# A softmax over 32768 columns on one core: other rows per partition, other statistics, other DMA pieces

## The chip, the core and the metric

One of the eight cores of a Trainium2 chip runs the whole program. The time is device microseconds (us) from start to end of one execution. Before the change, ten executions gave a median of 2504.91 us, from 2501.88 to 2509.04 us.

Names used below: DVE is the vector engine, ACT the scalar engine, SP the engine that issues the DMAs here, and a DMA is a transfer between the chip's main memory and the on-chip memory of 128 partitions. A DMA is carried out by 16 DMA engines at once.

## The reference

```python
batch, seq, vocab = 16, 256, 32768          # logits, float32; temperature = 1.0
scaled = logits / temperature
scaled = scaled - scaled.max(axis=-1, keepdims=True)
exp_scaled = np.exp(scaled)
return (exp_scaled / exp_scaled.sum(axis=-1, keepdims=True)).astype(np.float32)
```

There are 4096 rows of 32768 numbers, 128 KB each: 536.87 MB to read and as much to write.

## The kernel before

The input is cut into 128 tiles of 4 MB. A tile is 32 whole rows: each row is cut into four quarters of 8192 columns, and each quarter (32 KB) lies on one partition, so partition p of a tile holds the p-th stretch of 32 KB of 4 MB that are contiguous in main memory. `_BUFS` = 6 such tiles fit on the chip at once.

`load` (L49 to L54) and `store` (L56 to L59) each issue one DMA of 4 MB from SP's queue. `keep_in_program_order` fixes their order to what the last loop writes (L134 to L140): four loads (`_AHEAD` = 4), then, for each tile, its store and the load of the tile four later. SP works through its queue in this order, so a DMA that has to wait holds back all later ones. A load waits until the store that last used its buffer has landed; a store waits until the tile is finished.

`compute` (L74 to L132) works on a tile in two chunks of 4096 columns (`NCH` = 2):

- DVE finds the negated maximum of each chunk (L87), and ACT computes the exponential of the chunk in place with that maximum, and its sum on the way (L94).
- The small part (L103 to L125) joins the two chunks of a partition and then the four partitions of a row. `combine` (L61 to L72) does the latter in `n_rounds` = 2 rounds of a shuffle among 32 partitions (L64) and a `tensor_tensor` (L67); it is called once for the maximum and once for the sum. ACT computes the correcting exponentials (L106), DVE the weighted sum (L113) and the reciprocal (L124), and ACT the final factors (L125).
- The chunk is multiplied by its factor: of eight chunks in turn three on DVE (L130) and five on ACT (L132).

Which engine does which work is written out in the code. The order within DVE's and ACT's queues is set by a scheduler, and the small part is marked `high_priority`.

Of the kernel before, what the change touches and what calls it, by code (L numbers as in the profile page):

```python
# [1 line left out]

# [4 lines left out]


_W = 8192
_BUFS = 6  # L10
_AHEAD = 4
_CC = 4096
_SCALE_ON_DVE = {1, 4, 7}


@with_exitstack
def kernel(
    ctx: ExitStack,
    tc: tile.TileContext,
    logits: bass.AP,  # L20
    temperature: bass.AP,
    out: bass.AP,
):
    nc = tc.nc
    inv_t = 1.0 / float(temperature)
    P = nc.NUM_PARTITIONS
    fp32 = mybir.dt.float32
    Exp = mybir.ActivationFunctionType.Exp
    Copy = mybir.ActivationFunctionType.Copy
    X = mybir.AxisListType.X  # L30
    A = mybir.AluOpType

    xf = logits.flatten_outer_dims()
    of = out.flatten_outer_dims()
    N, V = xf.shape
    W = min(_W, V)
    SPLIT = V // W
    assert SPLIT * W == V and (N * SPLIT) % P == 0 and W % _CC == 0
    x = xf.rearrange("n (h v) -> (n h) v", h=SPLIT)
    o = of.rearrange("n (h v) -> (n h) v", h=SPLIT)  # L40
    n_tiles = N * SPLIT // P
    n_rounds = SPLIT.bit_length() - 1
    NCH = W // _CC

    xpool = ctx.enter_context(tc.tile_pool(name="x", bufs=_BUFS))
    spool = ctx.enter_context(tc.tile_pool(name="stats", bufs=8))
    slots = {}

    def load(t: int) -> None:  # L49
        xs = xpool.tile([P, W], fp32, tag="x", name="xs")  # L50
        slots[t] = xs
        tc.keep_in_program_order(
            nc.sync.dma_start(out=xs, in_=x[t * P : (t + 1) * P, :])
        )  # L54

    def store(t: int) -> None:  # L56
        tc.keep_in_program_order(
            nc.sync.dma_start(out=o[t * P : (t + 1) * P, :], in_=slots.pop(t))  # L58
        )  # L59

    def combine(v, op) -> None:  # L61
        for j in range(n_rounds):
            mask = [i ^ (1 << j) for i in range(32)]
            nc.vector.stream_shuffle(  # L64
                out=v[:, j + 1 : j + 2], in_=v[:, j : j + 1], mask=mask
            )
            nc.vector.tensor_tensor(  # L67
                out=v[:, j + 1 : j + 2],
                in0=v[:, j : j + 1],
                in1=v[:, j + 1 : j + 2],  # L70
                op=op,
            )  # L72

    def compute(t: int) -> None:  # L74
        xs = slots[t]
        nm = spool.tile([P, NCH], fp32, tag="nm", name="nm")
        ssum = spool.tile([P, NCH], fp32, tag="ssum", name="ssum")
        ee = spool.tile([P, NCH], fp32, tag="ee", name="ee")
        f = spool.tile([P, NCH], fp32, tag="f", name="f")
        ttj = spool.tile([P, NCH], fp32, tag="ttj", name="ttj")  # L80
        nMh = spool.tile([P, 1 + n_rounds], fp32, tag="nMh", name="nMh")
        Sh = spool.tile([P, 1 + n_rounds], fp32, tag="Sh", name="Sh")
        rS = spool.tile([P, 1], fp32, tag="rS", name="rS")

        for c in range(NCH):
            xc = xs[:, c * _CC : (c + 1) * _CC]
            nc.vector.tensor_reduce(  # L87
                out=nm[:, c : c + 1], in_=xc, axis=X, op=A.max, negate=True
            )
            if inv_t != 1.0:  # L90
                nc.vector.tensor_scalar_mul(
                    out=nm[:, c : c + 1], in0=nm[:, c : c + 1], scalar1=inv_t
                )
            nc.scalar.activation(  # L94
                out=xc,
                in_=xc,
                func=Exp,
                bias=nm[:, c : c + 1],
                scale=inv_t,
                accum_out=ssum[:, c : c + 1],  # L100
            )

        with tc.high_priority():  # L103
            nc.vector.tensor_reduce(out=nMh[:, 0:1], in_=nm, axis=X, op=A.min)  # L104
            combine(nMh, A.min)
            nc.scalar.activation(  # L106
                out=ee,
                in_=nm,
                func=Exp,
                bias=nMh[:, n_rounds : n_rounds + 1],  # L110
                scale=-1.0,
            )
            nc.vector.tensor_tensor_reduce(  # L113
                out=ttj,
                in0=ee,
                in1=ssum,
                scale=1.0,
                scalar=0.0,
                op0=A.mult,
                op1=A.add,  # L120
                accum_out=Sh[:, 0:1],
            )
            combine(Sh, A.add)
            nc.vector.reciprocal(out=rS, in_=Sh[:, n_rounds : n_rounds + 1])  # L124
            nc.scalar.activation(out=f, in_=ee, func=Copy, scale=rS)  # L125

        for c in range(NCH):
            xc = xs[:, c * _CC : (c + 1) * _CC]
            if (t * NCH + c) % 8 in _SCALE_ON_DVE:
                nc.vector.tensor_scalar_mul(out=xc, in0=xc, scalar1=f[:, c : c + 1])  # L130
            else:
                nc.scalar.activation(out=xc, in_=xc, func=Copy, scale=f[:, c : c + 1])  # L132

    for t in range(min(_AHEAD, n_tiles)):  # L134
        load(t)
    for t in range(n_tiles):
        compute(t)
        store(t)
        if t + _AHEAD < n_tiles:
            load(t + _AHEAD)  # L140


# [1 line left out]
_INS = ['logits', 'temperature']  # L144
_OUTS = [((16, 256, 32768), 'float32')]

_NUMBERS = {'temperature': 1.0}


# [26 lines left out]
```

## Time and profile before

| what | before |
|---|---|
| median of ten executions | 2504.91 us |
| the profiled execution's own time | 2509.04 us |
| its span, from the first instruction to the last | 2507.3 us |
| instructions | 4102 |
| maximum of 128x4096, DVE (L87) | 4414 ns, 256 times |
| exponential of 128x4096, ACT (L94) | 3707 ns, 256 times |
| multiplication of 128x4096, ACT (L132) | 3705 ns, 160 times |
| multiplication of 128x4096, DVE (L130) | 2353 ns, 96 times |
| one load or store | 4096 KB, 128 of each |
| one packet of a DMA engine | 32768 bytes, 1213 ns (median) |

The span is what the trace covers; the execution's own time is 1.7 us longer. The profiled execution is also the slowest of the ten, 4.1 us above their median. In a line of the costliest groups the name is followed by the tiles that are written and read, the shape, the count, the busy time in us, the mean of one in ns, and the idle time of the engine just before such an instruction, with what ended it. In a line of waits, the engine and line that waited stand to the left of the arrow, and what they waited for to its right. Every DMA consists of packets[...], and the trace has the start and the length of each packet. It also has the moment at which each of the 16 DMA engines finished its part of a DMA.

### The profile page before, as it was taken

The numbers are of one execution on the slowest core, as the hardware profiler recorded it, in microseconds if no ns is written. First come the engines' busy times: TensorE is split into PE (matmuls) and PEld (weight loads), VectorE is DVE, ScalarE is ACT, GpSimd is POOL, SyncE is SP. The second block draws the span as 40 slices with busy tenths as digits, with TensorE's granted clock in tenths as the row PEclk, the third lists the DMA queues.
The fourth block names the chain that finished last, engine by engine and source line by source line (L and its number), as shares of the span: only waits on it lengthen the run. The fifth ranks groups of instructions, "written<-read, shape, count | busy, mean of one in ns | idle before, by whom it ended". The sixth has DMA issues, their size and how long they took to land.

```text
span 2507.3 us, 4102 instructions
## 1 busy us (share of the span) xinstructions
DVE 1564.3 (62%) x2400; ACT 1624.9 (65%) x929; POOL 0.2 (0%) x4
## 2 busy tenths in 40 slices
DVE  6666566666566666666666666566666666666664
ACT  6766666666666666666666666666666666666664
POOL 0000000000000000000000000000000000000000
DMA  9999999999999999999999999999999999999996
GB/s 410 432 433 434 431 432 433 435 434 431 433 433 433 434 432 431 434 434 434 432 431 434 432 434 431 431 434 433 435 431 432 434 434 434 432 431 435 432 434 273
DMA packets 36896, 1074.02 MB, mean 428 GB/s; under 512 B 4096, under 2 KB 4096, under 8 KB 4096
## 3 DMA queue, kind: packets, MB, share of 16 engines
q1 hardware_dynamic: 36864, 1073.76, 99.3%
q14 instruction: 32, 0.26, 0.0%
HBM read 536.87 MB, written 536.87 MB: 428 GB/s over the span
## 4 chain that ended last, share of the span: by engine, by line
DMA 73%; DVE 12%; ACT 9%; another core or an unknown queue 5%; issue 0%; SPq 0%; ACTq 0%
DMA xs<-in_logits_dram 47%; DMA out_dram<-xs 25%; DVE nm L87 10%; ACT xs L94 4%; ACT xs L132 4%; DVE Sh L67 0%; DVE Sh L64 0%; ACT f L125 0%; DVE xs L130 0%; ACT ee L106 0%; DVE rS L124 0%; DVE ttj L113 0%; SPq L58 0%; DVE nMh L67 0%
## 5 line engine op out<-in xcount | busy, mean ns | idle before, releaser
L87 DVE TENSOR_REDUCE nm<-xs 128x1 f32<-128x4096 f32 x256 | 1119.6, 4414 | 439.2 <-DMA xs<-in_logits_dram 439.2
L94 ACT ACTIVATE xs<-xs,nm 128x4096 f32<-128x4096 f32 x256 | 949.1, 3707 | 684.1 <-DVE nm L87 684.1
L132 ACT ACTIVATE xs<-xs,f 128x4096 f32<-128x4096 f32 x160 | 589.9, 3705 | 4.1
L113 DVE CUSTOM_DVE_ANT_0 ttj<-ee,ssum 128x2 f32<-128x2 f32 x128 | 20.5, 160 | 391.7 <-ACT ee L106 383.1
L130 DVE TENSOR_SCALAR xs<-xs,f 128x4096 f32<-128x4096 f32 x96 | 225.9, 2353 | 41.0 <-ACT f L125 41.0
L125 ACT ACTIVATE f<-ee,rS 128x2 f32<-128x2 f32 x128 | 37.8, 295 | 159.1 <-DVE rS L124 159.1
L94 ACT ACTIVATION_READ_ACCUMULATOR xs<-xs,nm 128x1 f32 x256 | 47.7, 187 | 0.0
L67 DVE TENSOR_TENSOR nMh<-nMh 128x1 f32<-128x1 f32 x256 | 40.8, 159 | 8.6
L67 DVE TENSOR_TENSOR Sh<-Sh 128x1 f32<-128x1 f32 x256 | 40.8, 159 | 8.6
L64 DVE STREAM_SHUFFLE nMh<-nMh 128x1 f32<-128x1 f32 x256 | 38.8, 151 | 0.0
L64 DVE STREAM_SHUFFLE Sh<-Sh 128x1 f32<-128x1 f32 x256 | 38.8, 151 | 0.0
L106 ACT ACTIVATE ee<-nm,nMh 128x2 f32<-128x2 f32 x128 | 35.8, 280 | 0.0
L124 DVE RECIPROCAL rS<-Sh 128x1 f32<-128x1 f32 x128 | 21.0, 164 | 4.3
L104 DVE TENSOR_REDUCE nMh<-nm 128x1 f32<-128x2 f32 x128 | 19.8, 155 | 4.3
L113 DVE DVE_READ_ACCUMULATOR2_ANT Sh<- 128x1 f32 x128 | 10.6, 83 | 0.0
L64 DVE LOAD_MASK_SELECT Sh<-Sh x256 | 3.6, 14 | 10.8
L64 DVE LOAD_MASK_SELECT nMh<-nMh x256 | 3.6, 14 | 10.7
L94 ACT ACT_TABLE_LOAD x1 | 1.3, 1283 | 12.9 <-DMA xs<-in_logits_dram 12.9
L157 POOL MEMSET const-bfloat16-1.0<- 128x1 bf16 x1 | 0.1, 102 | 0.0
L157 POOL MEMSET const-uint8-127<- 128x1 uint8 x1 | 0.1, 102 | 0.0
L157 POOL MEMSET const-float32-0.0<- 128x1 f32 x1 | 0.1, 99 | 0.2 <-issue 0.2
L157 POOL MEMSET const-float32-1.0<- 128x1 f32 x1 | 0.1, 99 | 0.0
## 6 DMA issues: line engine op xcount, KB each, us to landing
xs<-in_logits_dram SPq DMA_DIRECT2D x128, 4096.0 KB, 48.8
out_dram<-xs SPq DMA_DIRECT2D x128, 4096.0 KB, 49.6
```

Of the source, the lines that this page charges most:

```text
L64: nc.vector.stream_shuffle(out=v[:, j + 1 : j + 2], in_=v[:, j : j + 1], mask=mask)
L67: nc.vector.tensor_tensor(out=v[:, j + 1 : j + 2], in0=v[:, j : j + 1], in1=v[:, j + 1 : j + 2], op=op,)
L87: nc.vector.tensor_reduce(out=nm[:, c : c + 1], in_=xc, axis=X, op=A.max, negate=True)
L94: nc.scalar.activation(out=xc, in_=xc, func=Exp, bias=nm[:, c : c + 1], scale=inv_t, accum_out=ssum[:, c : c + 1],)
L104: nc.vector.tensor_reduce(out=nMh[:, 0:1], in_=nm, axis=X, op=A.min)
L106: nc.scalar.activation(out=ee, in_=nm, func=Exp, bias=nMh[:, n_rounds : n_rounds + 1], scale=-1.0,)
L113: nc.vector.tensor_tensor_reduce(out=ttj, in0=ee, in1=ssum, scale=1.0, scalar=0.0, op0=A.mult, op1=A.add, accum_out=Sh[:, 0:1],)
L124: nc.vector.reciprocal(out=rS, in_=Sh[:, n_rounds : n_rounds + 1])
L125: nc.scalar.activation(out=f, in_=ee, func=Copy, scale=rS)
L130: nc.vector.tensor_scalar_mul(out=xc, in0=xc, scalar1=f[:, c : c + 1])
L132: nc.scalar.activation(out=xc, in_=xc, func=Copy, scale=f[:, c : c + 1])
L157: nc = _bacc.Bacc("TRN2", target_bir_lowering=False, num_devices=1)
```

## The change

- A partition now holds half a row (64 KB, `_SPLIT` = 2) in two chunks of 8192 columns. A chunk of 128 half rows is still 4 MB and still one buffer of six. Two chunks form a group of 8 MB (64 rows), and the small part runs once per group, with one round in `combine`.
- The order of the rows on the partitions is new: partition p = 8 x (2s + h) + b holds half h of row 8b + s of the group. In main memory, the step from b to b + 1 is 1 MB, and the step from one of the 16 values of (s, h) to the next is 64 KB. The DMA's access pattern has the three steps (16, 8, columns) on the side of main memory.
- The maximum and the exponential cover 8192 columns in one instruction. The multiplication of each chunk is cut in two halves of 4096 columns, one for DVE and one for ACT. The final factors are computed on DVE instead of ACT.
- Six loads come first instead of four. The store of chunk i stands ahead of the load of chunk i + 5, which takes the buffer of chunk i - 1.
- In the first group the loads, and in the last group the loads and the stores, are cut into pieces of 4096 columns. In the last group the instructions are cut in the same way.

```diff
-_W = 8192
+_SPLIT = 2
+_OUTER = 16
+_INNER = 8
+_CW = 8192
 _BUFS = 6
-_AHEAD = 4
-_CC = 4096
-_SCALE_ON_DVE = {1, 4, 7}
+_PIECE = 8192
+_LAST_DMA = 4096
+_DVE_SHARE = 0.5
...
-    x = xf.rearrange("n (h v) -> (n h) v", h=SPLIT)
+    W = V // _SPLIT
+    CW = min(_CW, W)
+    C = W // CW
+    x = xf.rearrange(
+        "(g b s) (h v) -> g (s h) b v", h=_SPLIT, b=_INNER, s=_OUTER // _SPLIT
+    )
...
+    def piece(g: int) -> int:
+        return _PIECE if g < G - 1 else min(_PIECE, _LAST_DMA)
+
+    def load(i: int) -> None:
+        g, c = divmod(i, C)
+        xs = xpool.tile([P, CW], fp32, tag="x", name="xs")
+        slots[i] = xs
+        for s, n in spans(CW, _LAST_DMA if g in (0, G - 1) else CW):
+            tc.keep_in_program_order(
+                nc.sync.dma_start(
+                    out=xs[:, s : s + n],
+                    in_=x[g, :, :, c * CW + s : c * CW + s + n],
+                )
+            )
...
-            mask = [i ^ (1 << j) for i in range(32)]
+            mask = [i ^ (_INNER << j) for i in range(32)]
...
-            nc.scalar.activation(out=f, in_=ee, func=Copy, scale=rS)
-
-        for c in range(NCH):
-            xc = xs[:, c * _CC : (c + 1) * _CC]
-            if (t * NCH + c) % 8 in _SCALE_ON_DVE:
-                nc.vector.tensor_scalar_mul(out=xc, in0=xc, scalar1=f[:, c : c + 1])
-            else:
-                nc.scalar.activation(out=xc, in_=xc, func=Copy, scale=f[:, c : c + 1])
-
-    for t in range(min(_AHEAD, n_tiles)):
-        load(t)
-    for t in range(n_tiles):
-        compute(t)
-        store(t)
-        if t + _AHEAD < n_tiles:
-            load(t + _AHEAD)
+            nc.vector.tensor_scalar_mul(out=f, in0=ee, scalar1=rS)
+
+    def scales(i: int) -> None:
+        g, c = divmod(i, C)
+        xs = slots[i]
+        f = stats[g][3]
+        ps = spans(CW, piece(g))
+        for j, (s, n) in enumerate(ps):
+            k = c * len(ps) + j
+            cut = int(n * _DVE_SHARE) // 512 * 512
+            nc.vector.tensor_scalar_mul(
+                out=xs[:, s : s + cut], in0=xs[:, s : s + cut], scalar1=f[:, k : k + 1]
+            )
+            nc.scalar.activation(
+                out=xs[:, s + cut : s + n],
+                in_=xs[:, s + cut : s + n],
+                func=Copy,
+                scale=f[:, k : k + 1],
+            )
+
+    order = [("L", i) for i in range(min(_BUFS, n_chunks))] + [("S", 0)]
+    for i in range(1, n_chunks):
+        order.append(("S", i))
+        if i + _BUFS - 1 < n_chunks:
+            order.append(("L", i + _BUFS - 1))
...
+    for kind, i in order:
+        if kind == "L":
+            load(i)
+            loaded = i + 1
+        else:
+            g = i // C
+            if g > done:
+                while nxt < (g + 1) * C:
+                    assert nxt < loaded
+                    exps(nxt)
+                    nxt += 1
+                factors(g)
+                done = g
+            scales(i)
+            store(i)
```

## The prediction

> **What bounds the kernel now.** I read the page first: its busy shares, its slices and its DMA queues.
>
> ```profile
> span 2507.3 us, 4102 instructions
> ...
> DVE 1564.3 (62%) x2400; ACT 1624.9 (65%) x929; POOL 0.2 (0%) x4
> ...
> GB/s 410 432 433 434 431 432 433 435 434 431 433 433 433 434 432 431 434 434 434 432 431 434 432 434 431 431 434 433 435 431 432 434 434 434 432 431 435 432 434 273
> ...
> q1 hardware_dynamic: 36864, 1073.76, 99.3%
> q14 instruction: 32, 0.26, 0.0%
> ```
>
> Both compute engines idle for a third of the time, while the DMAs move 431 to 435 GB/s in every slice but the first and the last. A DMA engine's packet of 32 KB takes 1213 ns and the next starts 1209.4 ns after it (starts of the packets in the trace): 32768 bytes x 16 / 1209.4 ns = 433 GB/s. The DMAs are the bound, and each engine already runs without a pause. Next I asked for the DMAs alone, from 60 to 2440 us, and for busy time in stretches at the end:
>
> ```profile
> q14 instruction: 30, 0.25, 0.0%
> issues: line engine op xcount, KB each, median us to landing
> out_dram<-xs SPq DMA_DIRECT2D x123, 4096.0 KB, 49.6
> xs<-in_logits_dram SPq DMA_DIRECT2D x122, 4096.0 KB, 49.0
> ```
> ```profile
> 2466.00:2476.00 10.00, 8.91 (x5) 4.01 (x3) 0.00 (x0) 1.00 0.98 423
> 2476.00:2485.00 9.00, 3.92 (x16) 7.70 (x5) 0.00 (x0) 1.00 0.11 47
> 2485.00:2495.00 10.00, 0.00 (x0) 0.09 (x1) 0.00 (x0) 1.00 0.97 417
> 2495.00:2497.00 2.00, 0.00 (x0) 0.00 (x0) 0.00 (x0) 1.00 0.08 33
> 2497.00:2507.00 10.00, 0.00 (x0) 0.00 (x0) 0.00 (x0) 1.00 0.05 23
> ```
>
> The second last number of a stretch is the mean share of the 16 DMA engines. In the last 10 us it is 0.05, about one engine of 16: the others had finished near 2497. From 2476 to 2485, too, little more than one engine works, while the others wait for the last store. So **one DMA engine sets the end**. The moments at which the 16 engines finish their part of each DMA show how it got there (us; lag is the distance to the median engine):
>
> ```
> DMA ends at   lag of the last   lag of the second last
>      65.6          2.4                2.1
>     554.6          7.1                4.1
>    1197.8         11.5                4.1
>    1845.3         19.9                6.2
>    2352.1         23.4                9.0
> ```
>
> The last engine's lag grows in steps of 0.7 to 1.1 us, and these fall on instruction fetches (queue 14, 8 KB each): at 298, 435, 552, 688, 805, 942, 1065, 1194 us and on, 20 in all. Behind such a fetch (309 ns) one data packet takes some 1790 instead of 1213 ns, so a fetch costs the engine about 0.9 us. 4102 instructions / 32 fetches = 128 each; DVE has 20 x 128 of them, so I take these 20 for DVE's. The others (nine of ACT's pace, three of SP's) don't move the last engine's lag.
>
> The last engine's account: first packet at 3.0 us; 2048 packets (256 DMAs x 8) x 1.2094 = 2476.9; 20 fetches x 0.94 = 18.8; the remainder, 8.6, is slow packets (some 5 before 143 us, the rest near 1250 to 1590 us). Sum 2507.3.
>
> [...]
>
> **The change, part by part.**
>
> *Fewer instructions.* The built programs have, with the second instruction of each shuffle and each exponential counted, 2500 before and 1035 after on DVE, 1188 and 657 on ACT, 398 and 526 on SP. At 128 per fetch that is 20 and 8 fetches for DVE, 9 and 5 for ACT, 3 and 4 for SP. The last engine saves 12 x 0.94 = **11.3 us**. It stays the last: ACT's engine was 13.7 us ahead of it at the end and loses four fetches itself.
>
> *Compute, with cover.* Per 8 MB, DVE has four maxima's worth (4 x 4.41), two multiplications (2 x 2.35) and about 2 of small work: 24.4 us. ACT has 4 x 3.71 + 2 x 3.71 + 1 = 23.3. The DMAs need 4 x 9.68 = 38.7 for the same, so I cost all of it at nothing. Moving the factors to DVE and halving the multiplications falls under this too.
>
> *The group of two chunks, SP's order.* A load of chunk i + 5 now waits for the landing of store i - 1. While it waits, the next store stands behind it on SP. When it is released, the last DMA engine still has one load and one store ahead of it, 19.4 us of work; I therefore expect loads to land about 29 us after issue and stores about 39. Before, SP waited for this as well:
>
> ```profile
> SPq L53 <- DMA out_dram<-xs: 1170.9, 119, 11.6
> SPq L58 <- DVE xs L130: 604.0, 90, 6.9
> SPq L58 <- ACT xs L132: 470.5, 120, 14.6
> ```
>
> Is the store ready by then? After the second chunk of a group has landed: maximum 8.8, exponential 7.4, small part 2.5, multiplication 3.7, together 22.4 us. Its SP turn comes 29 us after that landing (store, load, store). It is 6.6 us early, and if late, has another 19.4 us before the ring is empty. Cost nothing; without the cover it would be 64 groups x the gap.
>
> *First and last pieces.* At the start the ring holds six loads (58 us), and the first store is ready at about 45: no gap, but no gap before either. At the end, three stores (29 us) now lie between the last load and its own store, so the other engines' 9 us gap closes; but the last engine was never idle there for more than a fraction, so closing it gains nothing. [...]
>
> *The addresses.* The packets remain 32 KB. From below: [...] the early slow packets are the only thing to win, 0 to 5 us in total. [...] I take nothing[...].
>
> **Sum.** Span 3.0 + 2476.9 + 8 x 0.94 + 8.6 = 2496.0 us; profiled time 2497.7. Against the profiled 2509.04 this is -11.3; against the median of 2504.91, which lies 4.1 lower, it is **2493.6 us**. With the remainder between 2.5 (what the median engine lost) and 13, this case reaches from 2487 to 2498.
>
> **The rivals.** A difference within 0.2% (5 us) is about what can't be told from no change.
>
> *The gain is used up in small gaps.* The prefetch is shorter (two DMAs queued in place of four at each release), so engines that run ahead by more than 19.4 us run dry, and stray slow packets, such as the 5 us of the first 143, can come back in each group. 64 groups x 0.18 us = 11.3 gives 2505 us. For it: slow packets appeared when DMAs changed places early on. Against it: the lag of the last engine should be near 13, below 19.4.
>
> *The packets get slower (slower than before).* The place is the 16 x 8 pattern. [...] It decides from 11.3 / 2048 = 5.5 ns per packet, 0.46%. For it: the pattern is new[...]. Against it: before, 16 engines spread over a 4 MB tile reach the full rate, and one DMA still covers every partition. If it comes, I give half of its chance to times below 2545, around 2520.
>
> *The change does less than it says*[...]: this is part of my forecast.
>
> **Chances.** Forecast 0.60; used up 0.10; slower packets 0.30. The range takes the forecast's lower end, 2487, and reaches to 2545, which leaves out half of the slower case (0.15) and little else. Faster 0.60, within 0.2% 0.10, slower 0.30. The forecast's own range is 2487 to 2498.
>
> **What would show it.** Right: 16 to 18 instruction packets in queue 14 instead of 32; packets of 32 KB still at 1213 ns and slices at 431 to 435 GB/s; a lag of the last engine of 11 to 14 us at the end instead of 23; the last 10 us again with one busy DMA engine; loads landing after some 29 us; no 9 us hole before the last store. Wrong: slices below 430 GB/s or packets above 1219 ns (slower packets); or a last engine whose lag is as large with half the fetches, which would mean that fetches only coincide with its steps.

## The result, and the profile after

| | before | after |
|---|---|---|
| median | 2504.81 us (29 executions, 2501.88 to 2509.9) | 2621.08 us (8 executions, 2616.52 to 2628.72) |
| ratio after / before | | 1.0466, 95% interval 1.0456 to 1.0475 |
| the profiled execution's span | 2507.3 us | 2653.7 us |
| instructions | 4102 | 2234 |

The change makes the kernel 4.7% slower, where 0.45% faster was forecast; the time lies outside the stated range. The profiled execution of after is 34 us above its median, and above all eight executions of the table; why it is longer than they are isn't shown, because only this one has a trace. Ratios, here and below, are worked out without executions that lie over 1.5% above the fastest of the same kernel.

The page of after, in its busy shares, slices, queues and DMA issues (name, count, size of one, median us from issue to landing):

```profile
span 2653.7 us, 2234 instructions
...
DVE 1487.8 (56%) x964; ACT 1405.2 (53%) x455; POOL 0.2 (0%) x4
...
GB/s 206 229 265 354 328 390 413 423 431 430 433 434 432 432 433 432 433 434 430 433 431 433 432 431 430 432 430 430 433 430 431 429 430 433 435 433 433 430 374 254
...
q1 hardware_dynamic: 37728, 1073.76, 99.6%
q14 instruction: 17, 0.14, 0.0%
...
out_dram<-xs SPq DMA_DIRECT2D x126, 4096.0 KB, 38.0
xs<-in_logits_dram SPq DMA_DIRECT2D x124, 4096.0 KB, 29.1
```

Much of the forecast is there: 17 instruction packets, loads that land after 29.1 us, stores after 38.0, and 429 to 435 GB/s over most of the span. New are the start and the end. The first slice has half of the full rate, and the full rate is reached only in the ninth (a slice is 66.3 us). The last two slices fall to 374 and 254. A slice at rate r loses 66.3 us x (1 - r / 433): the first eight lose 131 us, the last two 36.

The stretches of after (duration, busy time of DVE, ACT and POOL, clock, mean share of the 16 DMA engines, GB/s) show that the engines aren't idle in this time:

```profile
0.00:57.00 57.00, 17.84 (x6) 13.60 (x4) 0.20 (x4) 1.00 0.99 209
57.00:100.00 43.00, 23.23 (x15) 24.11 (x10) 0.00 (x0) 1.00 1.00 208
100.00:150.00 50.00, 28.72 (x24) 29.12 (x9) 0.00 (x0) 1.00 0.99 242
150.00:200.00 50.00, 8.69 (x1) 7.21 (x2) 0.00 (x0) 1.00 1.00 275
200.00:250.00 50.00, 23.32 (x15) 20.34 (x6) 0.00 (x0) 1.00 0.97 387
250.00:300.00 50.00, 23.24 (x15) 20.45 (x8) 0.00 (x0) 1.00 1.00 284
300.00:350.00 50.00, 23.32 (x15) 24.98 (x9) 0.00 (x0) 1.00 0.99 375
...
400.00:450.00 50.00, 32.10 (x20) 23.05 (x8) 0.00 (x0) 1.00 1.01 412
...
1000.00:2400.00 1400.00, 836.15 (x537) 788.41 (x250) 0.00 (x0) 1.00 1.00 432
```

The share is 1.00 at 208 GB/s as at 432: the engines work all the time, and their packets take twice as long. The way up isn't steady (387, then 284, then 375). The trace's own packet times say the same. From 44 to 122 us, when only loads run, a packet of 32 KB takes 2513 ns on the mean (490 of 496 take 2300 to 2700); from 500 to 2400 us the mean is 1217 ns, against 1214 before. In between both sorts occur: of 111 packets from 123 to 135 us, 53 took about 1213 ns and 42 between 2100 and 2700.

At the end the loads run out (the last were issued at 2551.5 us), stores are left alone, and the rate falls again (same columns):

```profile
2550.00:2600.00 50.00, 30.32 (x33) 35.78 (x17) 0.00 (x0) 1.00 1.00 359
2600.00:2653.00 53.00, 0.00 (x0) 2.00 (x2) 0.00 (x0) 1.00 0.73 241
```

SP's wait is now nearly all that of the loads for the store that frees their buffer. The lines are those of before, of after, and of the kernel with its rows in order that follows, each over its whole span:

```profile
SPq L53 <- DMA out_dram<-xs: 1177.8, 121, 11.6
SPq L71 <- DMA out_dram<-xs: 2258.4, 122, 50.2
SPq L67 <- DMA out_dram<-xs: 2246.3, 122, 19.3
```

The longer sum is the new order of loads and stores, not the loss: the last of the three kernels waits as long, and is fast.

**What the theories were.** After the result I held that the 16 x 8 split is at fault, in that the DMA engines hinder each other with it (P in the expectations, where they use letters). P with phase supposes that engines no longer do so once they are out of step, P without phase that they still do. The rival was that the 1 MB steps are slow in main memory (M). A third came up on the way: engines hinder each other in pairs, and only while both of a pair move in the same direction, so that it recovers when one loads while the other stores (D). All of these were suppositions.

### The profile page after: what moved, and what is told of

The parts are those of the page before. It is cut to its first block, busy times and chain, and to the rows that moved or that the text cites. A ratio compares the mean times of both kernels' runs of the same rounds, so it can differ in the third digit from the quotient of the medians.

```text
span 2653.7 us, 2234 instructions
## 1 busy us (share of the span) xinstructions
DVE 1487.8 (56%) x964; ACT 1405.2 (53%) x455; POOL 0.2 (0%) x4
## 4 chain that ended last, share of the span: by engine, by line
DMA 87%; another core or an unknown queue 6%; DVE 2%; SPq 2%; ACT 1%; issue 0%; ACTq 0%; DVEq 0%
DMA out_dram<-xs 84%; DMA xs<-in_logits_dram 3%; DVE nm L114 2%; SPq L71 1%; ACT xs L121 0%; DVE xs L167 0%; ACT xs L170 0%; SPq L82 0%; ACTq L231 0%; DVE f L157 0%; DVE rS L156 0%; DVE Sh L94 0%; DVE Sh L91 0%; ACT ee L138 0%
## 5 line engine op out<-in xcount | busy, mean ns | idle before, releaser
L121 ACT ACTIVATE xs<-xs,nm 128x8192 f32<-128x8192 f32 (+1 forms) x130 | 912.1, 7016 | 1102.0 <-DVE nm L114 1102.0
L114 DVE TENSOR_REDUCE nm<-xs 128x1 f32<-128x8192 f32 (+1 forms) x130 | 1111.5, 8551 | 667.3 <-DMA xs<-in_logits_dram 667.3
L170 ACT ACTIVATE xs<-xs,f 128x4096 f32<-128x4096 f32 (+1 forms) x130 | 468.1, 3648 | 71.4 <-DVE f L157 71.4
L167 DVE TENSOR_SCALAR xs<-xs,f 128x4096 f32<-128x4096 f32 (+1 forms) x130 | 295.7, 2317 | 3.7 <-DVE f L157 1.7
L145 DVE CUSTOM_DVE_ANT_0 ttj<-ee,ssum 128x2 f32<-128x2 f32 x64 | 10.3, 161 | 423.8 <-ACT ee L138 423.8
L121 ACT ACTIVATION_READ_ACCUMULATOR xs<-xs,nm 128x1 f32 x130 | 24.2, 186 | 0.0
L138 ACT ACTIVATE ee<-nm,nMh 128x2 f32<-128x2 f32 x64 | 17.9, 279 | 0.0
L156 DVE RECIPROCAL rS<-Sh 128x1 f32<-128x1 f32 x64 | 10.5, 164 | 2.2
L94 DVE TENSOR_TENSOR Sh<-Sh 128x1 f32<-128x1 f32 x64 | 10.2, 159 | 2.2
L94 DVE TENSOR_TENSOR nMh<-nMh 128x1 f32<-128x1 f32 x64 | 10.2, 159 | 2.2
L91 DVE STREAM_SHUFFLE Sh<-Sh 128x1 f32<-128x1 f32 x64 | 9.7, 151 | 0.0
L91 DVE STREAM_SHUFFLE nMh<-nMh 128x1 f32<-128x1 f32 x64 | 9.7, 151 | 0.0
## 6 DMA issues: line engine op xcount, KB each, us to landing
xs<-in_logits_dram SPq DMA_DIRECT2D x124, 4096.0 KB, 29.1
```

Source lines behind the costliest of these rows:

```text
L91: nc.vector.stream_shuffle(out=v[:, j + 1 : j + 2], in_=v[:, j : j + 1], mask=mask)
L94: nc.vector.tensor_tensor(out=v[:, j + 1 : j + 2], in0=v[:, j : j + 1], in1=v[:, j + 1 : j + 2], op=op,)
L114: nc.vector.tensor_reduce(out=nm[:, k : k + 1], in_=xs[:, s : s + n], axis=X, op=A.max, negate=True)
L121: nc.scalar.activation(out=xs[:, s : s + n], in_=xs[:, s : s + n], func=Exp, bias=nm[:, k : k + 1], scale=inv_t, accum_out=ssum[:, k : k + 1],
L138: nc.scalar.activation(out=ee, in_=nm, func=Exp, bias=nMh[:, n_rounds : n_rounds + 1], scale=-1.0,)
L145: nc.vector.tensor_tensor_reduce(out=ttj, in0=ee, in1=ssum, scale=1.0, scalar=0.0, op0=A.mult, op1=A.add, accum_out=Sh[:, 0:1],)
```

## The experiments

**The order of rows alone undone.** Rows lie on the partitions in order; all else is as after.

```diff
-    x = xf.rearrange(
-        "(g b s) (h v) -> g (s h) b v", h=_SPLIT, b=_INNER, s=_OUTER // _SPLIT
-    )
...
+    x = xf.rearrange("(g r) (h v) -> g (r h) v", h=_SPLIT, r=P // _SPLIT)
...
-            mask = [i ^ (_INNER << j) for i in range(32)]
+            mask = [i ^ (1 << j) for i in range(32)]
```

> The changed kernel with the half rows on the partitions in their order in main memory (a step of 64 KB from partition to partition, one step instead of the pattern of 16 x 8); all else stays. Theory P [...]: the first slices run at 410 GB/s or more instead of 206 to 265, the hole at the end goes too, and the forecast's sum holds: 2494 us, with the last engine's lag near 13 us. Theory M (main memory dislikes the addresses, steps of 64 KB and 1 MB): the 1 MB steps go and the 64 KB steps stay, so part of the slow start stays; 2510 to 2620 us. If the fetches of instructions did not cause the last engine's lag (rival to F, the theory that they do): full rate, but 2503 to 2507 us and a lag above 20.

Measured: 2494.8 us (2494.5 to 2497.09), ratio to before 0.9964 (0.995 to 0.9978). The page's slices and queue:

```profile
span 2492.7 us, 2234 instructions
...
GB/s 412 428 430 431 430 432 433 433 434 432 434 431 434 433 434 432 433 432 434 432 435 431 435 431 435 431 436 431 435 432 435 432 435 431 435 431 436 431 432 381
...
q14 instruction: 17, 0.14, 0.0%
...
out_dram<-xs SPq DMA_DIRECT2D x126, 4096.0 KB, 38.3
xs<-in_logits_dram SPq DMA_DIRECT2D x124, 4096.0 KB, 29.0
```

Slow start and slow end are gone, and the forecast's time (2493.6) is there. So the loss of after, 2621.1 - 2494.8 = 126 us, belongs to the order of the rows, and so to the pattern that it gives the DMAs.

**The split alone, in the kernel before.** A tile's 16 groups of eight partitions are taken from 16 places that lie 512 KB apart; within eight partitions the memory is contiguous (32 KB steps). The output `o` is changed in the same way.

```diff
-    x = xf.rearrange("n (h v) -> (n h) v", h=SPLIT)
...
+    R = 8 // SPLIT
+    x = xf.rearrange("(T o q r) (h v) -> T q o (r h) v", h=SPLIT, r=R, q=2, o=16)
...
-            nc.sync.dma_start(out=xs, in_=x[t * P : (t + 1) * P, :])
+            nc.sync.dma_start(out=xs, in_=x[t // 2, t % 2])
```

> The kernel before with one edit: two neighbouring tiles share 8 MB so that a tile takes every second block of eight pieces of 32 KB, and its DMAs have a pattern of 16 x 8 steps that can't be merged into one. Each block of eight is contiguous (256 KB) and the blocks lie 512 KB apart; instructions, sizes and queues are those of before. P: the loads at the start run at 206 to 215 GB/s with packets of some 2430 ns, then the rate recovers; some 60 to 150 us are lost, 2565 to 2655 us. M: contiguous blocks and no step of 1 MB, so full rate from the start, 2500 to 2510 us.

Measured: 2585.24 us (2576.04 to 2594.51), ratio 1.0323 (1.0296 to 1.035). Its slices:

```profile
GB/s 205 267 334 417 431 431 433 431 430 424 431 428 427 425 409 432 433 432 434 431 434 432 434 432 432 433 432 433 432 436 431 434 432 433 433 432 433 432 435 258
```

The same half rate at the start, with no steps of 1 MB between neighbouring partitions. The split into 16 groups of eight is enough for it.

**In order, but 64 partitions at a time.** The in-order kernel, without pieces, each DMA cut into one for partitions 0 to 63 and one for 64 to 127.

```diff
+            for q in (0, 64):
+                tc.keep_in_program_order(
+                    nc.sync.dma_start(
+                        out=xs[q : q + 64, s : s + n],
+                        in_=x[g, q : q + 64, c * CW + s : c * CW + s + n],
+                    )
...
```

> The half rows in their order in main memory, as in the first of these runs, with each DMA cut in two: partitions 0 to 63, then 64 to 127. No pieces of 4096 columns. P[...] the start is again at half rate, 200 to 220 GB/s, although the addresses are as in the first run; 2540 to 2680 us. M: addresses as in the first run, so its time within 1%, and no slow start of its own.

Measured: 2631.18 us (2620.01 to 2646.41), ratio 1.051 (1.0472 to 1.0548). The slices begin as those of after do:

```profile
GB/s 208 226 272 410 430 431 431 431 432 433 433 429 432 433 434 431 433 433 432 429 427 428 433 430 422 429 432 431 429 429 430 412 419 430 427 428 427 428 433 263
```

The addresses in main memory are those of the fast in-order kernel, and there is no pattern of 16 x 8; what differs is that a DMA covers 64 partitions, with twice as many DMAs. The first slice has 208 GB/s against 412 at the same addresses, so the addresses alone don't make the half rate. That the limit lies on the side of the on-chip memory was my reading; the run doesn't show it.

**Steps of 2 and 4 MB, with fewer neighbouring partitions.** After, with 32 groups of four partitions (2 MB steps within a group) and with 64 groups of two (4 MB).

```diff
-_OUTER = 16
-_INNER = 8
+_OUTER = 32
+_INNER = 4
```

> The changed kernel with a pattern of 32 x 4 steps instead of 16 x 8 (64 KB from one of the 32 to the next, 2 MB inside). [...] as slow a start as with 16 x 8, 206 GB/s in the first slice, 2580 to 2700 us. If it is the 16 steps in themselves: 410 GB/s or more in the first slice.

> The changed kernel with 64 x 2 steps (64 KB from one of the 64 to the next, 4 MB inside). The run with 32 x 4 had the full rate[...]. [...] 410 GB/s or more in the first slice, 2490 to 2500 us. If it was not the blocks that made 32 x 4 fast but the size of the step in main memory: the 4 MB steps bring a loss, above 2510 us.

Measured, one execution each: 2494.76 us and 2494.24 us. The slices of 32 x 4, then of 64 x 2:

```profile
GB/s 411 430 430 430 431 433 433 432 433 433 433 433 433 433 434 433 433 433 434 432 434 433 433 433 434 433 433 432 434 432 434 432 434 432 435 431 434 432 431 374
GB/s 412 429 433 429 433 431 433 432 434 433 433 433 433 433 434 433 433 432 435 432 434 432 434 432 433 433 433 433 433 434 432 434 432 434 433 433 432 435 429 377
```

Larger steps than those of after, a pattern of as many dimensions, and the full rate from the start. With the two experiments before, M is out. Of the three patterns only 16 x 8 is slow. Which partitions an engine gets, no trace tells. The slow start that the first half of the expectation for 32 x 4 has did not come.

**Two groups of engines out of step.** This tries P with phase. To the kernel of two halves one DMA of 1 MB (32 packets of 32 KB) was added at the start, meant to put eight of the engines four packets behind the others.

```diff
+    tc.keep_in_program_order(
+        nc.sync.dma_start(
+            out=spare[:32, :],
+            in_=xf.rearrange("(a n k) (h v) -> a k n h v", h=4, n=8, k=2)[0, 0],
+        )
+    )
```

> The run with two halves of 64 partitions, with one more DMA ahead of all others: 1 MB into partitions 0 to 31 with a pattern whose slowest step has 8 values[...]. Its data are overwritten by the sixth chunk's load before use. P with phase [...]: after some 10 us the full rate, above 410 GB/s in the first slices, and 2500 to 2515 us. P without phase [...] or M: no different from the run without the extra DMA.

Measured: 2644.26 us (2640.27 to 2686.12), ratio 1.0553 (1.0536 to 1.057). The landings show two groups of eight engines 5.5 to 7.3 us apart, as meant. The slices:

```profile
GB/s 195 212 266 365 411 409 425 428 427 432 432 432 433 432 432 433 433 432 433 432 431 429 432 429 432 433 433 433 433 432 427 431 431 429 435 431 434 432 430 207
```

The full rate from the start, which P with phase expects, did not come (195 GB/s in the first slice); it is the other half of the expectation that came.

The same with 2 MB, meant to put eight engines eight packets behind (the expectation calls one group of eight low, the other high):

```diff
-            out=spare[:32, :],
-            in_=xf.rearrange("(a n k) (h v) -> a k n h v", h=4, n=8, k=2)[0, 0],
+            out=spare[:64, :],
+            in_=xf.rearrange("(a n k r) (h v) -> a k n (r h) v", h=4, r=2, n=8, k=2)[0, 0],
```

> Two halves of 64 partitions, and ahead of all a DMA of 2 MB [...]. The count of engines that load at each moment has shown that the changed kernel recovers as it comes to eight loading and eight storing. D with pairs of one low and one high engine: as soon as stores join the loads, near 135 us, the rate is above 400 GB/s; 2560 to 2600 us. D with pairs inside the eight: no different from the halves without it, 240 to 300 GB/s until 200 us, 2620 to 2650 us.

Measured, one execution: 2944.13 us. Two groups of eight lie 18 us apart, so that for most of the time one loads while the other stores. The rate stays at or below 295 GB/s until about 960 us and reaches 426 only near 1180 us (a slice is 73.6 us):

```profile
GB/s 175 218 244 287 287 279 276 281 281 283 282 286 295 330 339 399 426 431 432 430 431 428 421 433 430 428 431 429 430 424 410 413 410 418 424 429 428 431 430 290
```

The time fits neither half of the expectation. The slow start fits partners that lie in the same group of eight. If so, neither run parted partners, the first doesn't refute P with phase, and by D the second made whole groups move in one direction and so prolonged the slowness.

**Loads alone.** The kernel of two halves out of step, without the multiplications and stores of all groups but the last.

```diff
+            if g == G - 1:
-            scales(i)
-            store(i)
+                scales(i)
+                store(i)
```

> The run with two halves of 64 partitions and the extra DMA that sets eight engines back by four packets, with the multiplications and the stores left out for all groups but the last; so for most of the run there are loads alone. P (phase): the skew, or drift, brings the loads to 400 GB/s or more within some 100 us; 1280 to 1400 us. D (direction): the loads stay at 208 GB/s to the end of them, 537 MB / 208 GB/s = 2580 us, whatever the phase.

Measured, one execution: 2650.28 us. Its slices:

```profile
GB/s 194 209 210 207 209 210 207 211 208 210 208 208 210 208 211 207 209 210 208 211 207 209 211 207 211 209 210 208 208 210 208 211 209 209 209 208 211 208 192 127
```

With loads only it never recovers in 2600 us. One engine falls behind its group of eight, by 5.4 us at 2000 us, some two of its packets (2430 to 2560 ns), and still no other engine gets ahead. Without stores there is no recovery, as D expected.

**One direction patterned, the other not.** After, with stores in row order (first) or loads in row order (second). The rows of the output then stand in another order than in the reference.

```diff
-    o = of.rearrange(
-        "(g b s) (h v) -> g (s h) b v", h=_SPLIT, b=_INNER, s=_OUTER // _SPLIT
-    )
+    o = of.rearrange("(g r) (h v) -> g (r h) v", h=_SPLIT, r=P // _SPLIT)
...
```

> The changed kernel with the 16 x 8 pattern in the loads alone; the stores use one step, so the rows of a group come out in another order than the reference's. P and D: the start is as slow as in the changed kernel (206 GB/s while only loads run), the end, where only stores run, is at 400 GB/s or more up to the last slice; 2570 to 2605 us. M (main memory): the slow start could only be due to reading; no difference from P and D in this run.

> The changed kernel with the 16 x 8 pattern in the stores alone; the loads use one step, so the rows of a group come out in another order than the reference's. P and D: the first slice, loads only, at 410 GB/s; a dip when the stores begin, near 60 us; the end slow as in the changed kernel (below 300 GB/s in the last slice, below 400 in the one before); 2530 to 2590 us. If stores are not hit at all: 2494 us.

Measured: four executions each, 3441 to 3631 us and 3205 to 3303 us. That is 28 to 45% longer than before, and both expectations missed by far. The slices of the first:

```profile
GB/s 211 285 298 332 317 296 303 307 316 309 325 319 319 298 291 292 292 296 311 299 293 290 291 290 290 289 288 288 287 292 291 292 291 291 288 287 292 291 294 303
```

By the landings of 500 to 3400 us, an engine takes 9.6 us (median) for its eight packets of a store, as at the full rate, and 19.2 for those of a load, as in the slow start. Together that is 28.8 us for the 8.39 MB of all engines, 291 GB/s, which is what the slices have. The recovery, then, isn't simply that stores run beside loads: where the loads are split 16 x 8 and the stores aren't, it doesn't come.

**Four engines late, within 16 x 8.** After without pieces, and one more DMA of 1 MB at the start whose slowest step is four, meant to put four engines eight packets behind.

```diff
+    tc.keep_in_program_order(
+        nc.sync.dma_start(out=spare[:32, :], in_=x[0, 0:4, :, 0:CW])
+    )
```

> The 16 x 8 pattern without pieces, with a DMA of 1 MB ahead of all that has four values in its slowest step[...]. [...] once stores join the loads (after some 140 us), [...] eight of the 16 landings of a DMA come well ahead of the others within 100 us, and the rate between 150 and 250 us is above the 245 to 280 GB/s that the run without the extra DMA has there. If the engines that share are others [...]: no group of eight pulls ahead, and it recovers as the run without it did.

Measured, one execution: 2602.99 us. The landings of its 16 engines (first the time in the span, then us after it; the last column counts engines):

```
DMA                  first lands at   then after                     engines
fifth of the loads       105.6        0.0 to 0.5 | 15.8 to 16.3       12 | 4
last before stores       125.5        0.0 to 0.6 |  7.8 to  8.1       12 | 4
the first store          135.1        0.0 to 0.2 | 3.7 to 4.6 | 11.4 to 12.1    4 | 8 | 4
a load of the next       161.7        0.0 to 0.2 | 9.0 to 15.4         4 | 12
```

While all load, the four stay 16 us behind and each of the 16 takes 20.1 us per load; being apart doesn't help. Once the twelve have gone over to stores, the four do the rest of their last load at twice the rate, and exactly four others get ahead of the remaining eight: they finish their first store in 9.6 us, the eight in 13 to 14. The reading that fits is that each of the late four has one partner among the twelve, and that both run at the full rate while one loads and the other stores. That is D, pair by pair, though the trace doesn't name the engines. The stretches (columns as above):

```profile
100.00:150.00 50.00, 32.29 (x20) 31.68 (x10) 0.00 (x0) 1.00 0.98 260
150.00:200.00 50.00, 14.17 (x10) 16.89 (x7) 0.00 (x0) 1.00 0.99 347
200.00:250.00 50.00, 26.73 (x16) 21.92 (x7) 0.00 (x0) 1.00 0.98 395
```

Without the extra DMA the three are 246, 307 and 417 in the kernel without pieces, and 242, 275 and 387 in after. So the gain from four engines is there at first and gone later. It is small beside what executions of one kernel differ by, so the landings are the evidence, not these rates. The expectation is met by half: four engines pull ahead, and not eight.

**Pieces left out of after.** `_LAST_DMA` is 8192.

> The changed kernel without the pieces of 4096 columns in the first and last group. Two theories of the recovery are left. P (phase): [...] the pieces cause the slow end (374 and 254 GB/s in the last two slices): the end gains 10 to 30 us, 2590 to 2610 us. D (direction): with this split loads alone, or stores alone, get about 208 GB/s whatever the phase, and the full rate comes only when half of the engines load while the other half store; then at the end, when only stores are left, the rate falls with or without pieces, and the time stays at 2615 to 2625 us.

Four executions gave 2605.89, 2677.02, 2680.55 and 2690.87 us, too far apart for a verdict. The profiled one (2605.89) has the same slow start, and its last slice is at 262 GB/s: the rate falls at the end without pieces too.

**Pieces left out of the in-order kernel.** The same edit there.

> The half rows in their order in main memory, without the pieces of 4096 columns in the first and last group. By the forecast's step on the pieces they gain nothing, because the DMA engines are never idle there: 2494 to 2497 us. If they shorten the start or the end: 5 to 15 us more, 2500 to 2510 us.

Measured: 2493.89 us (2493.55 to 2494.23), ratio 0.9953 (0.994 to 0.9967). Pieces gain nothing. This simplest version is 0.5% faster than before and 4.9% faster than after.

**The price of instructions.** Before, with ten multiplications of one column more per tile, 1280 in all.

```diff
+        more = spool.tile([P, 10], fp32, tag="more", name="more")
+        for j in range(10):
+            nc.vector.tensor_scalar_mul(
+                out=more[:, j : j + 1], in0=nm[:, 0:1], scalar1=2.0
+            )
```

> The kernel before with ten more small multiplications (one column each) on DVE per tile, 1280 in all, whose results nobody uses. F (each fetch of 128 DVE instructions costs the last DMA engine some 0.94 us): 10 more fetches, +9.4 us, 2514 us, 42 instruction packets and a last lag of some 33 us. If the fetches only coincide with the lag: DVE has 943 us of idle time, 1280 x 0.16 us = 205 us fit in; 2503 to 2507 us.

Measured: 2515.05 us (2512.62 to 2517.53) against 2504.77, ratio 1.0037 (1.0024 to 1.0049), +10.3 us.

```profile
span 2510.8 us, 5382 instructions
...
q14 instruction: 42, 0.34, 0.0%
```

Ten fetches more, 1.03 us each, and DVE is idle over a third of the time either way (busy 63% here, 62% before). In the trace the last engine's lag behind the median engine steps up at 29 of DVE's 30 fetches, by 0.6 to 1.3 us each (the thirtieth lies among the last stores). The steps add up to 26.2 us, and the lag near the end is 25.0, less than the 33 expected: before, the same fetches make up 18.7 us of 23.3, and the other 4.6, from slow packets elsewhere, is missing here. The two profiled executions differ by 3.6 us only, being the slowest of ten before and the fastest of five here. So medians and steps confirm the price of a fetch and its place; the lag at the end alone would not.

**How the recovery looks.** The order of loads and stores on each engine is taken to be that in which SP issued them, so that each landing tells what the engine does next. Engines that load, of 16, mean and standard deviation over a stretch (the column "two halves" is the kernel with each DMA cut in two):

```
stretch, us     before       after       rows in order   two halves
50 to 100      9.1  7.4    16.0  0.0      6.9  7.8       16.0  0.0
150 to 200     9.0  6.9    10.8  6.0      6.6  7.4       10.3  5.8
200 to 250     7.2  6.9     7.8  2.6      9.0  7.4        8.0  1.7
450 to 500     6.9  6.4     8.1  1.6      9.0  6.8        7.7  2.4
500 to 1000    8.0  6.1     8.1  1.6      7.9  6.8        8.0  2.2
```

Kernels at the full rate from the start swing between all loading and all storing. Those that recover have eight engines loading and eight storing nearly all the time (after: 6 to 10 of them in 94% of the time from 500 to 1000 us), and the rate comes back as this number settles. An even mix isn't enough, however: with two groups 18 us apart 10.1 engines load on the mean (standard deviation 1.7) from 500 to 1000 us, and with only the loads split 16 x 8 10.5 (1.9) from 1000 to 2000 us, at 276 to 330 and at some 290 GB/s. If D holds, it counts which engines load together, and not only how many.

## Why the prediction was wrong, point by point

- **The failing step** is "*The addresses.*", and in it "I take nothing". What happened is a factor of two: 2513 against 1213 ns a packet while only loads run. The row order alone costs 126 us of median. That the split of the partitions does it, and not the addresses, is shown by the split alone (205 GB/s in the first slice), by the two halves (208) and by the other two patterns (411 and 412). Which partitions an engine gets, and what engines share, is not shown.
- **Where the loss lies.** In the profiled executions after is 161.0 us longer than the in-order kernel (2653.7 - 2492.7). By the slices, the first eight lose 131 us in after and about 5 in the other, the last two 36 and about 8; the rest, some 7, is the middle at 431 to 432 instead of 433 GB/s. The six first loads alone, 25.2 MB, take 121 us at 208 GB/s instead of 58.
- **The rival that came true in part.** "The packets get slower" had the place (the 16 x 8 pattern), and ended on the right side. Its size was an estimate of mine and too small: half of its chance was for times below 2545, and the median is 2621.1. By D, what helps a pair is that one engine loads while the other stores, which can't begin before the first stores, and in after took until some 450 us to settle. A loss by large steps in main memory is refuted by steps of 2 and 4 MB at the full rate (432 to 435 GB/s in most slices), and by after itself, which moves 432 GB/s with its 1 MB steps once it has settled. That engines recover by being some packets apart was not shown: with the four late engines the distance was 16 us, 6.4 packets of 2.5 us, and no engine was faster than 20.1 us per load.
- **The sum without that step held, in part by luck.** It gave 2493.6; the kernel with rows in order has 2494.8, without pieces 2493.9. For the profiled execution it gave a span of 2496.0, and the in-order kernel has 2492.7: the lag was put too high, and the 4.1 us that the forecast took off, because the profiled execution of before is slower than its median, made up for that; in the in-order kernel the profiled execution is the fastest of four. Fewer fetches are a gain: 17 instead of 32, and ten more cost 10.3 us against 9.4 expected. In the in-order kernel six of DVE's eight fetches moved the last engine by 0.7 to 0.8 us rather than 0.94, the other two hardly, and it ends 6.6 us after the median engine, less than the 11 to 14 of the forecast. Loads landed after 29.0 us (29), stores after 38.3 (39).
- **Compute and the group of two chunks cost nothing**, as forecast: in-order slices are at 430 and more from the third to the last but one. The pieces gained nothing, as forecast. "The gain is used up in small gaps" (2505 us) did not come: the in-order kernel has no such gaps.

**What stays open.** What partners share is not shown; that there are pairs is inferred from the factor of two (2513 against 1213 ns) and from the four late engines, with which four others got ahead. The traces name no engine. Partners seem to lie within a group of eight in the two halves, and each of four late engines seems to have had its partner outside the four under 16 x 8. D doesn't cover all that the traces have: in the two halves, where all 16 engines go over from loads to stores in step, the first four packets of each took some 1.1 us apiece, and only the next four some 2.1 us. Why a pair whose loads are patterned and whose stores are not never recovers is not explained; nor is why drift leads pairs to opposite directions and how long that takes, which may be why executions of after differ. Whether pieces matter within 16 x 8 remains without a verdict.

## What to carry to other kernels

When DMAs bound a kernel, look at how a DMA's pattern splits the 128 partitions before looking at addresses: here 128, 64 x 2 and 32 x 4 ran at some 433 GB/s, 16 x 8 at 208 until loads and stores had mixed. A DMA share of 1.00 beside half the GB/s means longer packets, not idle engines, so compare packet times first (here 2513 against 1213 ns). And a pattern that no trace has shown yet has no measured price: "I take nothing" was a guess, and the row order cost 126 us.

## What the runs showed that I had not expected

- A DMA rate that recovers by itself: 208 GB/s with loads alone, 432 after some 450 us with loads and stores, with about eight engines loading and eight storing, and lower again (359, then 241 with some engines finished) as the loads run out and only stores are left.
- The same split in one direction only is worse than in both: about 296 GB/s with patterned loads, 325 with patterned stores, over the whole span, against 405 for after.
- Instructions cost time even on an engine that is idle a third of the time: 1280 small ones on DVE made a DMA-bound kernel 10.3 us longer, about 1 us per fetch of 8 KB.
